# Layer-1 output projection takes its convolution half first; weights of the output and latent stages split at set places; later transposes of maxima; thinner column sums

## The chip, the cores and the metric

One core of one Trainium2 chip. The metric is device time in microseconds (us) of one execution; before the change the median of three runs is 2918.06 us (2916.81 to 2920.32).

## The reference, cut to what matters

Two encoder layers over 2048 tokens of width 1024. What the change touches is layer 1: the latent projections with a norm, eight heads of attention over all tokens, and the output projection of two normed halves, then a layer norm and a gated embedding. (What the program calls the convolution half is the second half of the projection's rows; in layer 1 it holds the result `yd` of the gated chunks.)

```python
cq, ckv, kr, du, dv, z = _split(x @ w_in, ODD_SIZES)
q = (rms_norm(cq, q_norm) @ w_uq).reshape(Bn, S, C_HEADS, C_NOPE + C_ROPE)
kv = (rms_norm(ckv, kv_norm) @ w_ukv).reshape(Bn, S, C_HEADS, C_NOPE + C_V)
...
yc = mla_attention(q_nope, q_rope, k_nope, k_rope, v)      # softmax over all 2048 keys
yd = chunked_spatial_gate(jax.nn.gelu(du), jax.nn.gelu(dv), v_ln_g, v_ln_b, w_s, b_s)
y = jnp.concatenate([rms_norm(yc, c_norm), rms_norm(yd, d_norm)], axis=-1) * jax.nn.silu(z)
...
h = layer_norm(DEEPNORM_ALPHA * x + y @ w_out, post_ln_g[i], post_ln_b[i])
x = h + jax.nn.sigmoid(h @ ple_gate[i]) * (p[i] @ ple_proj[i])
```

## The kernel before, in words

Every large product is made of three matmuls on operands that are split into a high and a low part (`mm3`, lines 77 to 79; for the embedding lines 89 to 91). `split` (lines 67, 68) makes the parts: ScalarE (ACT) copies the high part, and VectorE (DVE) or GpSimd (POOL) subtracts to get the low part. The program runs in five stages: layer-0 projections with windowed attention (0 to 715 us of the span), `phase_out(0)` (to about 1125), `phase_c` (the layer-1 projections, to 1681), `phase_d` (attention, 1681 to 2451) and `phase_out(1)` (to the end).

**Latents** (`part_m`, from 1345 us). Eight small weight tiles (`wuq` six times, `wuk`, `wuv`) are loaded and split before the loop over four latent blocks, whose ScalarE work (lines 1003 to 1005) frees the PSUM buffers `pl` that TensorE (PE) fills.

**Attention** (`phase_d`). 32 blocks (8 heads, 4 chunks of 512 queries), called 0 to 31 here, each with 16 key steps `kb`. A step is three score matmuls into `pst`, one matmul `pm` (line 1166) for the maxima of the block after next, and two value matmuls (`px` line 1216, `py` line 1217) four steps behind; no values run at `kb` 4 and two pairs run at `kb` 5. ACT makes the exponential and `ph`, DVE the low part `pl` (line 1289) and the maximum over `pm` (line 1167), POOL adds `ph` into `acc` (line 1295). At `kb` 2 (`MAX_AT`) the maxima of the next block are transposed (`pmt`, line 1176), through a buffer of the same two-deep PSUM ring `C` that `pm` uses. At `kb` 15 the sums are read back and inverted (`rec`, lines 1252, 1253). In eight blocks a weight tile for the output stage is split at `kb` 13. PE follows the order written out here (`manual_schedule`); a scheduler sets that of the other engines, and each engine is in order.

**Output stage** (`phase_out(1)`). For each of 16 tiles of 128 tokens: `fetch` loads parts of the attention result (`yc`, `ycm`, `rec`) and the finished second half (`ou1`); `prep` (lines 604 to 615) joins and scales the first half, sums its squares over features (`colsum`, line 517: one matmul per 128 columns against a 128x128 tile of ones) and takes the root (`rms`, lines 99 to 105 on one element per row); `first` (from line 617) projects both halves, attention half first, and DVE adds them to `ox` (line 626), then layer norm (POOL lines 634, 635); `second` transposes (`pht`, line 648) and makes `pp` and `pg` (line 89). `ycm`, `rec`, weight tiles `wraw` and `praw` share a ring `rr` of three buffers. `prep(0)` is called at `kb` 2 of the last block, and the last two tiles of `w_out` and all eight of `ple_gate` are loaded around the end of attention.

Once attention is over `ps_open("pse")` lays PSUM out anew with three buffers in ring `C`.

Of the kernel before, what the change touches and what calls it, by code (L numbers as in the profile page):

```python
# [20 lines left out]
P = 128  # L21
# [6 lines left out]
EPS = 1e-6  # L28
BIG = 1e35
LAG = 4  # L30
MAX_AT = 2
SUM_AT = 9
WEIGHT_AT = 13
START_AT = 2
VW = 130
ATTEND = 4000
# [17 lines left out]
class Builder:  # L54
# [20 lines left out]
    def mm3(self, ps, ah, al, bh, bl, start, stop):  # L75
        mm = self.nc.tensor.matmul
        mm(ps, ah, bh, start=start, stop=False)  # L77
        mm(ps, ah, bl, start=False, stop=False)  # L78
        mm(ps, al, bh, start=False, stop=stop)  # L79

    def mm3s(self, ps, a, b, cols):

# [473 lines left out]
    def phase_out(self, layer, es=None, wo=None, w_out=None, w_pr=None, right=None):  # L556
# [8 lines left out]
        w_out = w_out or []  # L565
        wo = wo + self.out_rings(es, f"ow{layer}", range(len(wo), 4), right)
# [3 lines left out]
        xs, us, att, last = {}, {}, {}, {}  # L570
        OU = 3

        def fetch(t):
# [25 lines left out]
        def prep(t):  # L599

            if layer == 0:
                return
            yc, more, rec, sz = att.pop(t)
            u = us[t][0] = of.tile([P, 2, 4, P], F32R, name="ou0", tag="ou", bufs=OU)
            for a in range(2):
                nc.gpsimd.tensor_tensor(yc, yc, more[:, a], ALU.add)
            nc.vector.tensor_tensor(rec, yc, rec, ALU.mult)
            sq = more[:, 0]
            nc.scalar.activation(sq, rec, AF.Square)
            nc.vector.tensor_tensor(sz, rec, sz, ALU.mult)  # L610
            nc.gpsimd.tensor_tensor(sq[:, 0:2], sq[:, 0:2], sq[:, 2:4], ALU.add)
            nc.gpsimd.tensor_tensor(sq[:, 0], sq[:, 0], sq[:, 1], ALU.add)
            self.split(u[:, 0], u[:, 1], sz)
            self.colsum(ss[:, 0, t:t + 1], sq[:, 0], self.psC("cs"))
            self.rms(rs, ss, 0, slice(t, t + 1))

        def first(t):
            x, u = xs[t], us.pop(t)
            for h in range(2):
                for n in range(2):  # L620
                    ns = slice(n * 512, (n + 1) * 512)
                    ps = self.psA("py")
                    for k in range(4):
                        wh, wl = w_out[4 * h + k]
                        self.mm3(ps, u[h][:, 0, k], u[h][:, 1, k], wh[:, ns], wl[:, ns], k == 0, k == 3)
                    last[0] = nc.vector.scalar_tensor_tensor(x[:, ns], ps, rs[:, h, t:t + 1], x[:, ns],
                                                             ALU.mult, ALU.add)
            st = self.cp.tile([P, 20], F32, name="ost", tag="ost", bufs=3)
            for n in range(2):
                nc.vector.bn_stats(st[:, 6 * n:6 * n + 6], x[:, n * 512:(n + 1) * 512])  # L630
            nc.vector.bn_aggr(st[:, 12:14], st[:, 0:12])
            self.rsqrt(self.cp, st[:, 15:16], st[:, 13:14], 1.0, 0.5 * EPS, 1)
            nc.vector.tensor_scalar(x, x, st[:, 12:13], st[:, 15:16], ALU.subtract, ALU.mult)  # L633
            nc.gpsimd.tensor_tensor(x, x, lng, ALU.mult)  # L634
            nc.gpsimd.tensor_tensor(x, x, lnb, ALU.add)
# [41 lines left out]
                    self.dma(d["x1T"][ch, :, a, 4 * k4:4 * k4 + 4, tc_], xt[:, a])  # L677

        if right:
            fetch(0)  # L680
            fetch_x(0)
            w_out = w_out + self.out_weights(wo, I["w_out"][layer], range(len(w_out), 8))
            lng, lnb = self.out_norm(of, layer)
            prep(0)
            yield
            first(0)
            yield
            left = Ring(es, tc, f"ox{layer}l", 2)
            xr.pools += left.pools
        else:  # L690
            wp = self.out_rings(es, f"op{layer}", range(1))
# [82 lines left out]
    def phase_c(self):  # L774
# [191 lines left out]
        def part_m():  # L966
            ms = ExitStack()
            sp = ms.enter_context(tc.tile_pool(name="cm", bufs=1))
            lp, wl, qn, latp = lw
            wq = [None] * 6  # L970
            ring = Ring(ms, tc, "cmq", 6)
            for j in range(6):
                wq[j] = self.load_weight(rr, ring, I["w_uq"][j], f"wuq{j}").rearrange("p a (k m) -> p a k m", m=P)
            wk = self.load_weight(rr, Ring(ms, tc, "cmk", 1), I["w_uk"], "wuk").rearrange("p a (j m) -> p a j m", m=P)
            wv = self.load_weight(rr, Ring(ms, tc, "cmv", 1), I["w_uv"], "wuv")

            def st():
                return tr.tile([P, CH], F32, name="mst")
# [6 lines left out]
            def latents(ch):  # L985
# [7 lines left out]
                for b in range(4):  # L993
# [11 lines left out]
                    nc.scalar.activation(ps[:, lkv], ps[:, lkv], AF.Square, scale=128 ** -0.5, accum_out=sq[:, 0, 1:2])  # L1005
                    nc.gpsimd.tensor_copy(tok[:, 416:432], tok[:, 400:416])
                    nc.gpsimd.tensor_copy(tok[:, 432:448], tok[:, 384:400])
                    self.rsqrt(lp, sq[:, 1], sq[:, 0], 1.0, EPS, 2)
                    for i, cols in enumerate((lq, lkv)):
                        nc.vector.scalar_tensor_tensor(tok[:, cols], tok[:, cols], sq[:, 1, i:i + 1], qn[:, cols],  # L1010
                                                       ALU.mult, ALU.mult)
# [157 lines left out]
    def mla_max_end(self, blk):  # L1169
        nc, c = self.nc, self.c  # L1170
        h, qc = divmod(blk, 4)
        mx = self.mx.pop(blk)
        m = self.cp.tile([P, 4], F32, name="mxr", tag="mxr", bufs=2)
        nc.vector.tensor_reduce(m, mx, AX.X, ALU.max)
        ps = self.psC("pmt")
        nc.tensor.transpose(ps[0:4, 0:P], m, c["ident"])
        mt = self.cp.tile([4, P], F32R, name="mt", tag="mt", bufs=2)
# [13 lines left out]
    def phase_d(self):  # L1191
# [58 lines left out]
        def reciprocals(h, qc, rec):  # L1250
# [5 lines left out]
        weights, after = [], []  # L1256
        steps = chain(self.out_weight(out_wo, self.i["w_out"][1], range(6), after),
                      self.out_weight(out_wp, self.i["ple_proj"][1], range(2), after))
        with tc.manual_schedule(engines={mybir.EngineType.PE}):
            for blk in range(NBLK):  # L1260
                h, qc = divmod(blk, 4)
                qh, ql, kh, kl = self.mla_qk[h % 2]
                qs = slice(qc * CH, (qc + 1) * CH)
                loads = blk in range(6, 28, 3)
                if loads:
                    after.append(old[4])
                    next(steps)
                if blk == NBLK - 3:
                    right.close()
                    self.output = self.phase_out(1, out_es, out_wo, weights[:6], weights[6:], "right")  # L1270
# [6 lines left out]
                for kb in range(16):  # L1277
                    with tc.high_priority(100) if blk == 0 and kb < LAG else ExitStack():
# [27 lines left out]
                        if old is not None:  # L1306
                            if kb == LAG - 1:
                                finish(*old[:4])
                            if kb == SUM_AT - 2:
                                hl = sums(old[4], nc.gpsimd)  # L1310
                            if kb == SUM_AT:
                                rec = total(*old[:2], hl)
                            if kb == 15:
                                with tc.issue_after(behind.ins):
                                    reciprocals(*old[:2], rec)
                        if loads and kb == WEIGHT_AT:
                            with tc.issue_after(ex.ins), tc.issue_after(behind.ins):
                                weights.append(next(steps))
                old = (h, qc, x, y, acc)
            while queue:  # L1320
                values()
            finish(*old[:4])
            hl = sums(old[4], nc.vector)
            self.c_bufs = 3
            self.ps_open("pse")
# [102 lines left out]
```

## Time and profile before

| | before |
|---|---|
| median of three runs | 2918.06 us (2916.81 to 2920.32) |
| profiled execution | 2919.13 us, span 2917.3 us, mean granted clock 0.987 |
| PE busy | 2830.8 us (97%) |
| DVE / ACT / POOL busy | 68% / 45% / 37% |
| chain that ended last | PE 83%, DVE 6%, DMA 6% |

The span is the profiled time from the first instruction to the last; 1.8 us of the execution lie around it. Granted clock 1.00 stands for 2.4 GHz of PE and 0.50 for 1.2 GHz. With PE busy nearly all the time, the rest to be had is what PE waits for, the stretches at the lower clock, and the work itself.

### The profile page before, as it was taken

What the parts mean: (1) busy time and instruction counts of PE and PEld (TensorE: products, weight loads), DVE (VectorE), ACT (ScalarE), POOL (GpSimd) and SP (SyncE); (2) the same over time, 40 slices, a digit from 0 to 9 for tenths busy, and PEclk for the clock granted to TensorE, in tenths of its full rate; (3) what the DMA queues carried; (4) which work ended last, traced back from release to release, by engine and by line L of the source; (5) the groups of instructions that cost most, each with busy time, mean ns of one, the idle gap of its engine ahead of it and who ended that gap; (6) DMA issues with size and microseconds to landing.
All of it is one profiled execution on the core that took longest, in us unless ns stands there. A gap on an engine that the chain in (4) does not pass through costs nothing.

```text
span 2917.3 us, 38322 instructions
## 1 busy us (share of the span) xinstructions
PE 2830.8 (97%) x12808; PEld 2300.1 (79%) x12808; DVE 1993.4 (68%) x3957; ACT 1323.9 (45%) x2475; POOL 1092.1 (37%) x831
## 2 busy tenths in 40 slices
PE   8999999999999999999999999999999998999998
PEld 7888888887788888888888877777777775777777
DVE  3788457886744544455765689999898986655554
ACT  3545335544211112334442388888888885111111
POOL 0011000112311111120103078898989887333332
PEclk9999999999999999999999999999999998999999
DMA  7654365544544346325783233313332233433331
GB/s 231 183 141 141 126 195 162 144 123 147 184 128 124 116 140 241 99 70 188 265 290 80 73 84 75 83 35 73 93 84 56 53 95 103 110 103 115 98 116 40
DMA packets 316598, 365.26 MB, mean 125 GB/s; under 512 B 33248, under 2 KB 244368, under 8 KB 311280
## 3 DMA queue, kind: packets, MB, share of 16 engines
q1 hardware_dynamic: 288752, 333.38, 40.0%
q10 hardware_dynamic: 27648, 29.43, 2.9%
q8 instruction: 101, 1.65, 0.2%
q14 instruction: 97, 0.79, 0.1%
HBM read 238.19 MB, written 124.53 MB: 124 GB/s over the span
## 4 chain that ended last, share of the span: by engine, by line
PE 83%; DVE 6%; DMA 6%; ACT 2%; issue 2%; SPq 1%; POOL 1%; ACTq 0%; DVEq 0%; POOLq 0%
PE pg L89 7%; PE pa L78 6%; PE pa L79 6%; PE pa L77 6%; PE pg L91 4%; PE py L77 4%; PE pst L1281 4%; PE pst L1282 3%; PE py L78 3%; PE pst L1283 3%; PE pm L1166 3%; PE px L1216 3%; PE py L79 3%; PE py L1217 3%; PE pc L79 3%; PE pc L78 3%
## 5 line engine op out<-in xcount | busy, mean ns | idle before, releaser
L1295 POOL TENSOR_TENSOR acc<-acc,ph 128x512 f32<-128x512 f32 x448 | 583.1, 1302 | 52.7 <-ACT ph L1287 23.8
L1289 DVE TENSOR_TENSOR pl<-pst,ph 128x512 fp32r<-128x512 f32 x512 | 348.3, 686 | 62.5 <-ACT ph L1287 45.4
L1167 DVE TENSOR_REDUCE mx<-pm 128x1 f32<-128x512 f32 x512 | 348.5, 682 | 32.6 <-PE pm L1166 28.2
L77 PE MATMUL pa<-xh,w 128*128 128x512 f32 x832 | 327.9, 394 | 6.2 <-ACT xh L67 6.2
L78 PE MATMUL pa<-xl,w 128*128 128x512 f32 x832 | 328.7, 395 | 0.5 <-DVE xl L68 0.5
L1284 ACT ACTIVATE pst<-pst 128x512 f32<-128x512 f32 x512 | 296.3, 583 | 69.9 <-PE pst L1283 38.9
L79 PE MATMUL pa<-xh,w 128*128 128x512 f32 x832 | 327.7, 394 | 0.0
L1287 ACT ACTIVATE ph<-pst 128x512 fp32r<-128x512 f32 x512 | 301.0, 597 | 29.6 <-POOL acc L1295 0.4
L77 PE MATMUL py<-wh,ou 128*128 128x512 f32 x512 | 208.8, 408 | 19.4 <-ACT ou L67 7.8
L1281 PE MATMUL pst<-mqh,mkh 97*128 97x512 f32 x512 | 206.9, 404 | 10.9 <-DVE pl L1289 10.7
L1216 PE MATMUL px<-ph,mv 128*128 128x512 f32 x512 | 207.6, 405 | 3.0 <-ACT ph L1287 3.0
L634 POOL TENSOR_TENSOR ox<-ox,ln_g 128x1024 f32<-128x1024 f32 x32 | 77.0, 2405 | 355.7 <-DVE ox L633 301.8
L658 ACT ACTIVATE osg<-pg 128x512 f32<-128x512 f32 x64 | 38.3, 598 | 374.7 <-PE pg L91 369.7
L78 PE MATMUL py<-wl,ou 128*128 128x512 f32 x512 | 206.4, 403 | 0.0
L1282 PE MATMUL pst<-mql,mkh 96*128 96x512 f32 x512 | 205.3, 401 | 0.0
L1283 PE MATMUL pst<-mqh,mkl 96*128 96x512 f32 x512 | 204.8, 400 | 0.0
L1217 PE MATMUL py<-pl,mv 128*66 128x512 f32 x512 | 204.1, 399 | 0.6 <-DVE pl L1289 0.6
L1166 PE MATMUL pm<-mkh,mqh 96*128 96x512 f32 x512 | 203.0, 397 | 0.2 <-ACT mt L1178 0.2
L89 PE MATMUL pg<-wh,oht 128*128 128x512 f32 x512 | 201.0, 392 | 0.9 <-ACT oht L67 0.9
L79 PE MATMUL py<-wh,ou 128*128 128x512 f32 x512 | 201.4, 400 | 0.0
L89 PE MATMUL pg<-wl,oht 128*128 128x512 f32 x512 | 200.1, 391 | 0.0
L77 PEld LDWEIGHTS pa<-xh,w 128*128 128x128 f32 x832 | 156.9, 189 | 37.1 <-ACT xh L67 6.9
(377 smaller groups left out, 6269.4 us busy)
## 6 DMA issues: line engine op xcount, KB each, us to landing
ou<-u SPq DMA_DIRECT2D x96, 256.0 KB
qw<-q SPq DMA_DIRECT2D x64, 256.0 KB
x1T<-oxt SPq DMA_DIRECT2D x64, 256.0 KB
cx<-x1T SPq DMA_DIRECT2D x16, 1024.0 KB
q<-st SPq DMA_DIRECT2D x32, 256.0 KB
u<-ua SPq DMA_DIRECT2D x32, 256.0 KB
wraw<-in_w_out SPq DMA_DIRECT2D x16, 512.0 KB
ox<-in_x SPq DMA_DIRECT2D x16, 512.0 KB
```

The costliest lines, as they stand in the source:

```text
L77: mm(ps, ah, bh, start=start, stop=False)
L78: mm(ps, ah, bl, start=False, stop=False)
L79: mm(ps, al, bh, start=False, stop=stop)
L89: mm(ps, a[:, 0, k], b[k][part][:, cols], start=k == 0 and part == 0, stop=False)
L1167: nc.vector.tensor_reduce(self.mx[blk][:, b, kc:kc + 1], ps, AX.X, ALU.max)
L1216: mm(x, v[:, kb, 0:P], ph, start=kb == 0, stop=kb == 15)
L1281: mm(ps, kh[0:97, ks], qh[0:97, qs], start=True, stop=False)
L1282: mm(ps, kh[0:96, ks], ql[0:96, qs], start=False, stop=False)
L1284: ex = nc.scalar.activation(ps, ps, AF.Exp, scale=scale)
L1287: nc.scalar.activation(ph, ps, AF.Copy)
L1289: behind = nc.vector.tensor_tensor(pl, ps, pf, ALU.subtract)
L1295: nc.gpsimd.tensor_tensor(acc, acc, pf, ALU.add)
```

## The change

- The transposes of maxima move from `kb` 2 to 5, the reciprocals from `kb` 15 to 14, the weight splits from `kb` 13 to 11; `mt` has one buffer instead of two.
- `colsum` multiplies by two columns of the ones and not by 128, so each output is 2 wide.
- `prep` writes the sum of squares to a tile `sqs` of its own; `colsum` and `rms` of layer 1 move from `prep` into `first`, between the halves; `first` takes the second half first in layer 1.
- The last two tiles of `w_out` are split in blocks 29 and 30 at `kb` 11; `prep(0)` is issued after the last block.
- The eight small latent weights are loaded ahead of everything else in `part_m`; one pair is split after each latent block of the first chunk.

```diff
-MAX_AT = 2
+MAX_AT = 5
 SUM_AT = 9
-WEIGHT_AT = 13
+REC_AT = 14
+WEIGHT_AT = 11
...
-            self.nc.tensor.matmul(ps[:, bl], src[:, bl], self.c["ones"], start=True, stop=True)
-        self.nc.vector.tensor_copy(out, ps.rearrange("p (b m) -> p b m", m=P)[:, 0:n, 0])
+            self.nc.tensor.matmul(ps[:, 2 * b:2 * b + 2], src[:, bl], self.c["ones"][:, 0:2], start=True, stop=True)
+        self.nc.vector.tensor_copy(out, ps[:, 0:2 * n].rearrange("p (b m) -> p b m", m=2)[:, :, 0])
...
+            sqs[t] = of.tile([P, P], F32, name="sqs", tag="sqs", bufs=1)
             nc.scalar.activation(sq, rec, AF.Square)
             nc.vector.tensor_tensor(sz, rec, sz, ALU.mult)
             nc.gpsimd.tensor_tensor(sq[:, 0:2], sq[:, 0:2], sq[:, 2:4], ALU.add)
-            nc.gpsimd.tensor_tensor(sq[:, 0], sq[:, 0], sq[:, 1], ALU.add)
+            nc.gpsimd.tensor_tensor(sqs[t], sq[:, 0], sq[:, 1], ALU.add)
             self.split(u[:, 0], u[:, 1], sz)
-            self.colsum(ss[:, 0, t:t + 1], sq[:, 0], self.psC("cs"))
-            self.rms(rs, ss, 0, slice(t, t + 1))
...
-            for h in range(2):
+            for h in (0, 1) if layer == 0 else (1, 0):
+                if layer == 1 and h == 0:
+                    with tc.issue_after(last[1].ins):
+                        self.colsum(ss[:, 0, t:t + 1], sqs.pop(t), self.psC("cs"))
+                    self.rms(rs, ss, 0, slice(t, t + 1))
...
         if right:
+            lng, lnb = self.out_norm(of, layer)
+            yield
             fetch(0)
             fetch_x(0)
-            w_out = w_out + self.out_weights(wo, I["w_out"][layer], range(len(w_out), 8))
-            lng, lnb = self.out_norm(of, layer)
+            yield
             prep(0)
...
+            raws = [rr.tile([P, 1024], F32, name="wur") for _ in range(3)]
+            wq, wkv, cuts = [], [], []
             for j in range(6):
-                wq[j] = self.load_weight(rr, ring, I["w_uq"][j], f"wuq{j}").rearrange("p a (k m) -> p a k m", m=P)
...
+                self.dma(r, I["w_uq"][j])
+                cuts.append((t, r))
...
             for _ in latents(0):
-                pass
+                with tc.issue_after(behind[0].ins), tc.issue_after(behind[1].ins):
+                    for t, r in cuts[:2]:
+                        self.split(t[:, 0], t[:, 1], r)
+                del cuts[:2]
...
-                loads = blk in range(6, 28, 3)
+                loads = blk in range(6, 28, 3) or blk in (NBLK - 3, NBLK - 2)
...
-                            if kb == 15:
+                            if kb == REC_AT:
...
             finish(*old[:4])
+            with tc.issue_after(behind.ins):
+                next(self.output)
             hl = sums(old[4], nc.vector)
             self.c_bufs = 3
             self.ps_open("pse")
```

On PE, steps `kb` 2 and 3 of an attention block before (first fence, the transpose follows `pm` of `kb` 2) and steps `kb` 4 and 5 now (second fence); `pst` are scores, `px` and `py` values.

```order
L1166 MATMUL pm<-mkh_14444,mqh_14436 128x512
L1176 MATMUL pmt<-ident,mxr 4x128
L1216 MATMUL px<-ph_17212,mv_13674 128x512
L1217 MATMUL py<-pl_17213,mv_13674 66x512
L1281 MATMUL pst<-mqh_13543,mkh_13551 128x512
```

```order
L1236 MATMUL py<-pl_17194,mv_13637 66x512
L1310 MATMUL pst<-mqh_13506,mkh_13514 128x512
L1311 MATMUL pst<-mql_13510,mkh_13514 128x512
L1312 MATMUL pst<-mqh_13506,mkl_13518 128x512
L1185 MATMUL pm<-mkh_14407,mqh_14399 128x512
L1310 MATMUL pst<-mqh_13506,mkh_13514 128x512
L1311 MATMUL pst<-mql_13510,mkh_13514 128x512
L1312 MATMUL pst<-mqh_13506,mkl_13518 128x512
L1185 MATMUL pm<-mkh_14407,mqh_14399 128x512
L1195 MATMUL pmt<-ident,mxr 4x128
L1235 MATMUL px<-ph_17211,mv_13637 128x512
L1236 MATMUL py<-pl_17212,mv_13637 66x512
```

The transpose moved three steps back in its block; the step ahead of it now has no value matmuls.

On DVE in the last block before: work of `prep(0)` (`ss`, `rsq`, `rs`) stands between the low parts `pl` of attention.

```order
L1289 TENSOR_TENSOR pl_23018<-pst,ph_23017 128x512
L518 COPY ss_9899<-cs 128x1
L99 TENSOR_SCALAR rsq<-ss_9899 128x1
L100 TENSOR_SCALAR rsq<-rsq 128x1
L101 TENSOR_SCALAR rs_9898<-rsq 128x1
L1289 TENSOR_TENSOR pl_23029<-pst,ph_23028 128x512
L103 TENSOR_TENSOR rsq<-rs_9898 128x1
L104 SCALAR_TENSOR_TENSOR rsq<-rsq 128x1
...
L104 SCALAR_TENSOR_TENSOR rsq<-rsq 128x1
L1289 TENSOR_TENSOR pl_23041<-pst,ph_23040 128x512
```

Now, on DVE after the last `pl` of attention (`acs` splits the last sums, `ou` is the low part of the first half of tile 0):

```order
L1318 TENSOR_TENSOR pl_23225<-pst,ph_23224 128x512
L608 TENSOR_TENSOR rec_23043<-yc,rec_23043 128x512
L612 TENSOR_TENSOR szt<-rec_23043,szt 128x512
L69 TENSOR_TENSOR acs<-acc,acs 128x512
L69 TENSOR_TENSOR ou_23247<-szt,ou_23247 128x512
L630 SCALAR_TENSOR_TENSOR ox_23051<-py,rs_9898,ox_23051 128x512 x2
L519 COPY ss_9899<-cs 128x1
L100 TENSOR_SCALAR rsq<-ss_9899 128x1
```

All of `prep(0)` on DVE and ACT moved behind the last `pl`; in the last two blocks only `pl`, `rec` and what belongs to attention stand on DVE.

On PE from the end of attention now (before, the first `py` read the first half of tile 0, and the sum `cs` of a tile stood a whole `first` ahead of that tile's matmuls). `ou_23048` is the second half of tile 0, `ou_23247` its first half, `ou_23428` the second half of tile 1; where "..." stands the 24 matmuls of a half go on.

```order
L1236 MATMUL py<-pl_23225,mv_14416 66x512
L78 MATMUL py<-wh_19421,ou_23048 128x512
...
L80 MATMUL py<-wh_22491,ou_23048 128x512
L518 MATMUL cs<-ones,sqs 128x2
L78 MATMUL py<-wh_16088,ou_23247 128x512
...
L80 MATMUL py<-wh_17749,ou_23247 128x512
L1259 MATMUL psum<-acs,ones 128x512
L1260 MATMUL psum<-acs,ones 128x512
L78 MATMUL py<-wh_19421,ou_23428 128x512
```

The half that needs no work of `prep` comes first, and the sum `cs` of a tile lies between its own halves.

## Rows read from the trace of the kernel before

**Rows 1.** Waits of PE, whole span: waiter, releaser, us in total, times, longest.

```profile
PE cs L517 <- POOL ycm L612: 17.5, 6, 5.3
PE pst L1281 <- DVE pl L1289: 10.7, 4, 5.8
PE pmt L1176 <- DVE mx L1167: 8.1, 19, 0.6
PE py L77 <- ACT ou L67: 7.8, 4, 2.0
PE pl L77 <- ACT pl L1005: 5.4, 2, 3.9
```

**Rows 2.** Stretches: length, busy us of PE, PEld, DVE, ACT, POOL, granted clock, DMA.

```profile
1731.00:2340.00 609.00, 601.45 (x2575) 458.22 (x2574) 553.28 (x914) 533.43 (x970) 545.22 (x427) 1.00 0.30 67
2387.80:2451.20 63.40, 50.70 (x176) 35.83 (x174) 37.64 (x61) 44.24 (x82) 52.41 (x43) 0.81 0.32 86
2451.20:2540.00 88.80, 77.27 (x320) 62.24 (x321) 59.16 (x134) 17.02 (x27) 36.96 (x22) 0.92 0.42 117
2540.00:2911.80 371.80, 352.58 (x1571) 287.84 (x1569) 204.23 (x542) 51.64 (x92) 112.83 (x72) 0.98 0.35 97
```

**Rows 3.** Timeline of the latents, ACT and PE: start, length, ..., idle before.

```profile
1354.86 0.42 ACT L67 ACTIVATE wuq<-wuq3r 128x256 fp32r<-128x256 f32 x1 [2.87 <-DMA wuq3r<-in_w_uq]
1364.91 0.71 PE L77 MATMUL pl<-wl,cx 128*128 128x416 f32 x1 [3.95 <-ACT pl L1005]
```

**Rows 4.** The line of the maxima (DVE 1167): one of those who waited for it.

```profile
  PEld pmt L1176: 18.2, 23
```

**Rows 5.** Timeline of steps 4 and 5 of an attention block.

```profile
1761.56 0.69 DVE L1167 TENSOR_REDUCE mx<-pm 128x1 f32<-128x512 f32 x1 [0.70 <-PE pm L1166]
1762.07 0.39 PE L1166 MATMUL pm<-mkh,mqh 96*128 96x512 f32 x1
1762.30 0.39 PE L1216 MATMUL px<-ph,mv 128*128 128x512 f32 x1
```

**Rows 6.** Timeline of blocks 30 and 31.

```profile
2396.77 0.69 DVE L607 TENSOR_TENSOR rec<-yc,rec 128x512 f32<-128x512 f32 x1 [3.72 <-DMA rec<-rec]
2398.85 0.80 PE L1281 MATMUL pst<-mqh,mkh 97*128 97x512 f32 x1 [2.61 <-DVE pl L1289]
2417.23 0.15 DVE L518 COPY ss<-cs 128x1 f32<-128x1 f32 x1
2426.15 0.70 DVE L105 SCALAR_TENSOR_TENSOR rs<-rsq,rs 128x1 f32<-128x1 f32 x1
2426.28 0.80 PE L1281 MATMUL pst<-mqh,mkh 97*128 97x512 f32 x1 [5.78 <-DVE pl L1289]
```

**Rows 7.** A stretch behind the wait of 2.61 us: length, PE busy, granted clock.

```profile
2398.80:2405.60 6.80, 6.72 (x15) 0.52 0.91 243
```

**Rows 8.** POOL's groups in attention: busy, mean ns of one, idle before.

```profile
L1295 POOL TENSOR_TENSOR acc<-acc,ph 128x512 f32<-128x512 f32 x448 | 583.1, 1302 | 52.7 <-ACT ph L1287 23.8 <-POOL acc L1295 0.4
L68 POOL TENSOR_TENSOR acs<-acc,acs 128x512 fp32r<-128x512 f32 x31 | 40.4, 1304 | 3.0 <-ACT acs L67 3.0
```

**Rows 9.** Weights `wraw` from 2380 us: gate loads, POOL's splits (min/median/max ns, first and last).

```profile
L73 SPq DMA_DIRECT2D wraw<-in_ple_gate x8: 332/339/464, 2411.7 to 2484.7; - x8
L68 POOL TENSOR_TENSOR wl<-wraw,wh x5: 2338/2405/2408, 2423.3 to 2489.6; 128x1024 fp32r<-128x1024 f32 x5
```

**Rows 10.** Timeline of the output stage on PE: a column sum, the first gate matmul.

```profile
2486.26 0.80 PE L517 MATMUL cs<-ones,ycm 128*128 128x128 f32 x2 [5.32 <-POOL ycm L612]
2495.78 0.39 PE L89 MATMUL pg<-wh,oht 128*128 128x512 f32 x1
```

**Rows 11.** Timeline of a run of column sums: weight loads and matmuls.

```profile
714.98 1.75 PEld L517 LDWEIGHTS cs<-ones,sqb 128*128 128x128 f32 x14
715.21 3.73 PE L517 MATMUL cs<-ones,sqb 128*128 128x128 f32 x32
```

**Rows 12.** A step of the root on DVE from 2451.6 us (min/median/max ns).

```profile
L103 DVE TENSOR_TENSOR rsq<-rs x45: 147/159/2395, 2465.8 to 2859.4; 128x1 f32<-128x1 f32 x45
```

More of the change, by code (lines that the diff above doesn't have):

```diff
@@ L78, in mm3 @@
         mm(ps, ah, bl, start=False, stop=False)
-        mm(ps, al, bh, start=False, stop=stop)
+        return mm(ps, al, bh, start=False, stop=stop)
     def mm3s(self, ps, a, b, cols):
@@ L564, in phase_out @@
         wo = wo or []
-        w_out = w_out or []
-        wo = wo + self.out_rings(es, f"ow{layer}", range(len(wo), 4), right)
+        w_out = [] if w_out is None else w_out
+        wo = self.out_wo = wo + self.out_rings(es, f"ow{layer}", range(len(wo), 4), right)
         kw = {"side": right} if right else {}
@@ L569, in phase_out @@
         xr = Ring(es, tc, f"ox{layer}", 1 if right else 3, right)
-        xs, us, att, last = {}, {}, {}, {}
+        xs, us, att, sqs, last = {}, {}, {}, {}, {}
         OU = 3
@@ L624, in first @@
                         wh, wl = w_out[4 * h + k]
-                        self.mm3(ps, u[h][:, 0, k], u[h][:, 1, k], wh[:, ns], wl[:, ns], k == 0, k == 3)
+                        last[1] = self.mm3(ps, u[h][:, 0, k], u[h][:, 1, k], wh[:, ns], wl[:, ns], k == 0, k == 3)
                     last[0] = nc.vector.scalar_tensor_tensor(x[:, ns], ps, rs[:, h, t:t + 1], x[:, ns],
@@ L969, in part_m @@
             lp, wl, qn, latp = lw
-            wq = [None] * 6
-            ring = Ring(ms, tc, "cmq", 6)
+            raws = [rr.tile([P, 1024], F32, name="wur") for _ in range(3)]
+            wq, wkv, cuts = [], [], []
             for j in range(6):
-                wq[j] = self.load_weight(rr, ring, I["w_uq"][j], f"wuq{j}").rearrange("p a (k m) -> p a k m", m=P)
-            wk = self.load_weight(rr, Ring(ms, tc, "cmk", 1), I["w_uk"], "wuk").rearrange("p a (j m) -> p a j m", m=P)
-            wv = self.load_weight(rr, Ring(ms, tc, "cmv", 1), I["w_uv"], "wuv")
+                t = sp.tile([P, 2, 256], F32R, name=f"wuq{j}")
+                r = raws[j // 4][:, 256 * (j % 4):256 * (j % 4 + 1)]
+                self.dma(r, I["w_uq"][j])
+                cuts.append((t, r))
+                wq.append(t.rearrange("p a (k m) -> p a k m", m=P))
+            for j, nm in enumerate(("w_uk", "w_uv")):
+                t = sp.tile([P, 2, 512], F32R, name=nm)
+                r = raws[2][:, 512 * j:512 * (j + 1)]
+                self.dma(r, I[nm])
+                cuts.append((t, r))
+                wkv.append(t)
+            wk, wv = wkv[0].rearrange("p a (j m) -> p a j m", m=P), wkv[1]
+            behind = {}
             def st():
@@ L1009, in latents @@
                     for i, cols in enumerate((lq, lkv)):
-                        nc.vector.scalar_tensor_tensor(tok[:, cols], tok[:, cols], sq[:, 1, i:i + 1], qn[:, cols],
-                                                       ALU.mult, ALU.mult)
+                        behind[1] = nc.vector.scalar_tensor_tensor(tok[:, cols], tok[:, cols], sq[:, 1, i:i + 1],
+                                                                   qn[:, cols], ALU.mult, ALU.mult)
                     pt = self.psC("plt")
@@ L1176, in mla_max_end @@
         nc.tensor.transpose(ps[0:4, 0:P], m, c["ident"])
-        mt = self.cp.tile([4, P], F32R, name="mt", tag="mt", bufs=2)
+        mt = self.cp.tile([4, P], F32R, name="mt", tag="mt", bufs=1)
         nc.scalar.activation(mt, ps[0:4, 0:P], AF.Copy, scale=-1.0)
@@ L1254, in reciprocals, with out_steps @@
             self.dma(d["rec"][h, qs].rearrange("(p j) -> p j", j=4), rec[:, 0])
-        weights, after = [], []
-        steps = chain(self.out_weight(out_wo, self.i["w_out"][1], range(6), after),
-                      self.out_weight(out_wp, self.i["ple_proj"][1], range(2), after))
+        w_out, w_pr, after = [], [], []
+        def out_steps():
+            for out, rings, src, ks in ((w_out, out_wo, self.i["w_out"][1], range(6)),
+                                        (w_pr, out_wp, self.i["ple_proj"][1], range(2)),
+                                        (w_out, None, self.i["w_out"][1], range(6, 8))):
+                for w in self.out_weight(rings or self.out_wo, src, ks, after):
+                    if w:
+                        out.append(w)
+                    yield
+        steps = out_steps()
         with tc.manual_schedule(engines={mybir.EngineType.PE}):
@@ L1263, in phase_d @@
                 qs = slice(qc * CH, (qc + 1) * CH)
-                loads = blk in range(6, 28, 3)
+                if blk == NBLK - 3:
+                    right.close()
+                    self.output = self.phase_out(1, out_es, out_wo, w_out, w_pr, "right")
+                    next(self.output)
+                loads = blk in range(6, 28, 3) or blk in (NBLK - 3, NBLK - 2)
                 if loads:
@@ L1317, in phase_d @@
                             with tc.issue_after(ex.ins), tc.issue_after(behind.ins):
-                                weights.append(next(steps))
+                                next(steps)
                 old = (h, qc, x, y, acc)
@@ L1322, in phase_d @@
             finish(*old[:4])
+            with tc.issue_after(behind.ins):
+                next(self.output)
             hl = sums(old[4], nc.vector)
```

5 lines of the change are left out of this document (1 added, 4 removed).

## The prediction

> **What bounds the kernel now.** I read the page first: TensorE (PE) is busy for 2830.8 of the 2917.3 us. Time can come from three places only: less work on PE, waits of PE, and stretches at the lower clock. The list of PE's waits tells who holds it up [rows 1], and the table of stretches tells how much a stage loses [rows 2]. In attention up to block 27 PE is busy for 601.45 of 609.00 us at a clock of 1.00, so it loses some 7.6 us there. From block 30 to the end of attention, 63.40 us, it is idle for 12.7 us, and the clock of 0.81 takes another 0.19 x 63.4 = 12.0: 24.7 us lost, 38.7 of work. In the output stage the first 88.8 us lose 11.5 + 0.08 x 88.8 = 18.6, the other 371.8 us lose 19.2 + 0.02 x 371.8 = 26.6: 45.2 together. The clock falls behind waits: after the one of 2.61 us [rows 6] the next 6.80 us ran at 0.52 [rows 7], which is the level of 1.2 GHz, so a wait of this size costs its length and some 3.3 us more. The waits of up to 0.6 us in attention [rows 1] leave the clock at 1.00 [rows 2].
>
> The sum is made against the profiled execution, 2919.1 us, which lies 1.1 us above the median of the runs.
>
> **Latents: -5.** ScalarE (ACT) stands in order behind weights that have not landed, 2.87 us for one alone, and PE then waits 3.95 us for a PSUM buffer that ACT should have freed [rows 3]; all such waits come to 5.4 us [rows 1]. The change issues the eight loads ahead of everything and places each pair of splits behind ACT's work of a latent block, so nothing of the block stands behind them. The splits are as many as before and lie beside the matmuls of the latent blocks. I take 5, the waits less a remainder, and nothing for the clock; ends: 0 (another load is late instead) and 8.
>
> **Maxima: -10.** At step 2 the transpose wants the PSUM buffer of `pm` from step 1, and VectorE (DVE), late from the reciprocals at the block's start, has not read it. The matmuls waited 8.1 us [rows 1], their weight loads 18.2 [rows 4]; I take 10, near the first, because PE works on while a load waits. At step 5 the buffer is that of step 4. DVE read it from 1761.56 to 1762.25, and PE's next place after `pm` of step 5 was 1762.30 [rows 5]: 0.05 us to spare, after a DVE wait for PE, so DVE had caught up. That margin is thin, because step 4 has no values. Moving the reciprocals to step 14 gives DVE one step more. If the margin fails, one DVE reduction of 0.69 us per block over 30 blocks is 20 us, which is the bad end (+10 on balance); the good end is -18. Moved weight splits and the single `mt` are hidden: POOL, ACT and DVE are busy for 545, 533 and 553 of 609 us [rows 2], and without that cover a POOL split costs 2.4 us [rows 9].
>
> **Blocks 30 and 31: -21.** `prep(0)` stands in the in-order queues here. DVE waited 3.72 us for the load of `rec`, and PE then 2.61 us for `pl`; the root (one element per row) ran from 2417.23 to 2426.85 on DVE, and PE waited 5.78 us behind it [rows 6]. All of that moves behind the last block, so these waits and the clock they cost go. POOL is late next: 30 additions at 1.30 and two `acs` at 1.30 [rows 8] are 41.7 us, and a weight split at 2.4 [rows 9] makes 44.1, against PE's 38.7. The values don't need these sums, and seven buffers of `ph` let POOL lag by some steps, so I put the pair of blocks at 42.4, between the two: 63.4 - 42.4 = 21. Ends: 25 (PE alone) and 13 (POOL sets the pace and its waits bring one fall of the clock). The two weight tiles in blocks 29 and 30 add a split each, beside matmuls.
>
> **Output stage: -27 of 45.** What PE waits for is `cs` behind POOL, 17.5 us, and `py` behind ACT's `ou`, 7.8 us [rows 1]. The first case is seen at 2486.26: `cs` of a tile stands on PE ahead of matmuls that don't need it, 5.32 us idle [rows 10]. Now the half that needs no `prep` comes first, which gives the sum and the split 24 matmuls, 24 x 0.23 = 5.6 us [rows 5], more; and `sqs` frees a buffer of the load ring sooner. In the first stretch I leave 9 of 18.6: POOL's lag of 2 to 3 us at the end of attention delays `acs`, behind which DVE has `ou` of tile 0, plus one wait for a load, plus one fall of the clock. The rest loses 26.6 in waits of about 2 us that return with the ring of three; I leave a third, 9. Gain 9.6 + 17.4 = 27. Ends: 10 (the loads are as late as before) and 44.
>
> **Column sums: 0.** 32 instructions took 3.73 us, 0.117 us each, while the weight loads came every 1.75/14 = 0.125 us without a gap [rows 11]. A thinner result shortens the streaming; the 128 columns of weights stay, and the loads alone fill the run. For all 128 such instructions the ends are 0 and 15 us, the whole run; I take 0, by the row of the loads. The Trainium skill (TensorE: Matmul & The Clock Gate, LDWEIGHTS) gives a load as its columns divided by 1.2, an estimate of 107 ns here, so it speaks against this edit: by that the sum would gain 128 x 0.010 = 1.3 us more. The run of 0.117 agrees.
>
> Sum: -5 - 10 - 21 - 27 + 0 = -63, so 2856 us. With every end at its best it is -95 (2824; with free column sums 2809), with every end at its worst -13 (2906).
>
> **Rivals.**
> 1. *The gate weights come late.* All eight loads of `ple_gate` now follow the end of attention; before they ran from 2411.7 to 2484.7 [rows 9], the first of them ahead of that end. They pass the ring of three beside `ycm` and `rec`. The first `pg` stood at 2495.78 [rows 10], 44.6 us after attention; now it is due after some six halves, about 36 us. If it comes no earlier than before, PE waits 8.6 us and the clock costs 3.3: 2868. For it: POOL's split of 2.4 us per tile [rows 9], and its lag. Against: DMA is busy for 0.42 of that stretch [rows 2].
> 2. *The margin at step 5 fails.* The maxima then give +10 in place of -10: 2876. For it: 0.05 us [rows 5]. Against: DVE had waited for PE there.
> 3. *Thin sums pay.* Were PE's loads hidden, up to 15 us: 2841. Against: the row of the loads [rows 11].
> 4. *Slower: the root in the middle of `first`.* It now stands on DVE between the halves, ahead of the addition of the first half and the split of `pht` that `pg` needs. From `cs` to that `pg` PE has 24 + 12 matmuls and 8 transposes, about 9.3 us; additions and splits take 2.8 of that on DVE, so it decides when the root takes over 6.5 us. It took 9.6 beside POOL's additions [rows 6]. Then each tile waits 3.1 us and pays 3.3 for the clock: 16 x 6.4 = 102, so 2958. Against: a step has a median of 159 ns [rows 12], which makes 2 us for twelve, and POOL is busy for a third of the stage; for it: single steps of 2395 ns, the length of a POOL operation. The Trainium skill (SBUF — State Buffer, Terms, "shared port pair") says that VectorE and GpSimd share a pair of ports under an exclusive lock, held for a whole instruction; by that rule any step with two inputs can be stalled, and the long steps in the row agree.
>
> **How the numbers follow.** The forecast has 0.5 (its own range 2842 to 2870), rival 1 0.2, rival 2 0.14, rival 3 0.11, rival 4 0.05. The forecast and rivals 1 to 3 lie between 2828 and 2884 with 8 in 10 of the chance when their own spread of some 12 us is counted; that is the range. About 0.2% (6 us) can be told from no change. Only rival 4 is slower; of its 0.05 the chance leaves 0.04 slower and 0.01 in a mild form that just uses up the gain, and 0.01 comes from all ends at their worst: faster 0.94, same 0.02, slower 0.04.
>
> **What would show it.** Right: no `pmt` wait in PE's list; no wait for `pl` above 1 us in the last two blocks, which take about 42 us; the output stage from the last value to the last matmul in some 433 us, with `cs` and `ou` below 10 us together; no `pl` wait in the latents; sums still about 0.11 us apart. Wrong: PE waits for `pg` weights or `ou` of over 5 us after attention, `pmt` waiting at its new place, or long root steps ahead of a PE wait in each tile.

## The result and the profile after

The changed kernel takes 2886.2 us (median, 2884.56 to 2887.82); the kernel before, timed beside it, 2919.2. The ratio is 0.9888 (95% interval 0.9871 to 0.9905): 33 us faster. The forecast was 2856 us with a range of 2828 to 2884, so the sign was right, the size about half, and the time lies 2 us outside the range.

The page after: span and busy times.

```profile
span 2885.3 us, 38365 instructions
...
PE 2820.2 (98%) x12808; PEld 2290.2 (79%) x12808; DVE 2014.4 (70%) x3957; ACT 1322.6 (46%) x2475; POOL 1091.2 (38%) x833
```

The waits of PE after, over the whole span (waiter, releaser, us in total, times, longest). Lines have moved: `cs` is line 518, the projections 78 to 80, the DVE addition 630.

```profile
PE py L78 <- DVE ox L630: 10.8, 7, 4.4
PE py L78 <- ACT ou L68: 7.5, 1, 7.5
PE pa L78 <- ACT xh L68: 7.0, 2, 5.0
PE py L78 <- DMA ou<-u: 6.6, 2, 4.0
PE pm L1185 <- DVE mx L1186: 3.5, 5, 1.4
PE py L80 <- DMA ou<-u: 2.6, 1, 2.6
PE psum L1259 <- ACT acs L68: 2.0, 1, 2.0
...
PE psum L1260 <- POOL acs L69: 1.6, 1, 1.6
```

Against [rows 1], the 17.5 us of `cs` are gone, and so are the 8.1 us of `pmt` for `mx`. New in layer 1 are one wait of 7.5 us for `ou` (the longest was 2.0) and waits of 6.5 us for loads of `ou` (the other 2.6 us lie in layer 0, as 3.2 us did before), and PE now stands at `psum` in the last block for 3.6 us where it stood 0.7. One wait of 1.8 us of `pmt`, for another releaser (`mxr`) and ahead of block 1, is left.

The stretches after that answer to [rows 2]: attention up to block 27; blocks 30 and 31; the first 88 us behind them; the rest up to the last matmul.

```profile
1731.00:2340.00 609.00, 604.57 (x2584) 458.46 (x2583) 552.84 (x919) 534.85 (x975) 549.42 (x429) 1.00 0.30 67
2381.10:2431.60 50.50, 44.19 (x174) 31.61 (x173) 26.91 (x45) 40.19 (x76) 48.82 (x39) 0.93 0.20 55
2431.60:2520.00 88.40, 68.79 (x273) 54.21 (x273) 59.19 (x133) 19.11 (x27) 42.86 (x27) 0.86 0.51 139
2520.00:2880.20 360.20, 356.69 (x1620) 292.88 (x1618) 244.89 (x562) 52.09 (x95) 108.73 (x72) 1.00 0.36 103
```

Read as before (idle time plus what the clock took), the first stretch of the output stage now loses 19.6 + 0.14 x 88.4 = 32 us where it lost 18.6, and the rest loses 3.5 us where it lost 26.6. So the stage became quiet in its steady part and worse at its start. In the two profiles, by the first score matmul of a block, the last value matmul and the last matmul of all (one profile of each kind; the experiments tell how far such a row can be trusted):

| stretch | before, us | after, us | difference | forecast |
|---|---|---|---|---|
| start to block 1 (latents lie here) | 1707.75 | 1704.67 | -3.1 | -5 |
| block 1 to block 30 (maxima) | 680.1 | 676.4 | -3.6 | -10 |
| blocks 30 and 31 | 63.3 | 50.3 | -13.0 | -21 |
| last value to last matmul | 460.5 | 448.5 | -11.9 | -27 |

**Blocks 30 and 31.** The timeline of POOL, ACT and PE in the last two blocks (start, us, engine, line, op; in brackets idle time before and releaser):

```profile
2399.37 2.40 POOL L69 TENSOR_TENSOR wl<-wraw,wh 128x1024 fp32r<-128x1024 f32 x1
2406.96 11.31 POOL L1324 TENSOR_TENSOR acc<-acc,ph 128x512 f32<-128x512 f32 x9
2416.45 0.63 ACT L68 ACTIVATE acs<-acc 128x512 fp32r<-128x512 f32 x1
2417.14 0.80 PE L1259 MATMUL psum<-acs,ones 128*128 128x512 f32 x1 [2.03 <-ACT acs L68]
2418.23 1.26 POOL L69 TENSOR_TENSOR acs<-acc,acs 128x512 fp32r<-128x512 f32 x1
2419.54 0.79 PE L1260 MATMUL psum<-acs,ones 128*128 128x512 f32 x1 [1.61 <-POOL acs L69]
```

Block 30 takes 19.54 us, all of it PE work; block 31 takes 30.8. POOL runs without a pause from the weight split to past the wait for its `acs` and falls behind. PE reaches `psum`, which wants the sums of block 30 at step 9 of block 31, and waits for POOL's `acs` with all later scores queued behind it. So some values did need these sums, by way of PE's order.

**The start of the output stage.** PE, ACT and DVE after attention:

```profile
2447.62 0.60 PE L78 MATMUL py<-wh,ou 128*128 128x512 f32 x1 [3.98 <-DMA ou<-u]
2466.26 2.30 DVE L106 SCALAR_TENSOR_TENSOR rs<-rsq,rs 128x1 f32<-128x1 f32 x1
2469.48 0.80 PE L78 MATMUL py<-wh,ou 128*128 128x512 f32 x1 [4.37 <-DVE ox L630]
2471.07 1.06 ACT L68 ACTIVATE wh<-wraw 128x1024 fp32r<-128x1024 f32 x1 [5.36 <-DMA wraw<-in_ple_gate]
2479.96 0.69 DVE L608 TENSOR_TENSOR rec<-yc,rec 128x512 f32<-128x512 f32 x1 [2.49 <-DMA rec<-rec]
2483.43 0.80 PE L78 MATMUL py<-wh,ou 128*128 128x512 f32 x1 [7.45 <-ACT ou L68]
2494.97 0.50 PE L80 MATMUL py<-wh,ou 128*128 128x512 f32 x1 [2.56 <-DMA ou<-u]
```

The second half of tile 1 has not landed when PE wants it (3.98 us). Then the addition `ox` is late (4.37 us): it stands on DVE behind the root of tile 1, which runs from 2458.05 to 2468.56 us, between other work and with steps of over 2 us. Then tile 2's `rec` comes late, its load issued at 2471.5, after the last of the eight gate weights, and `ou` of tile 2 with it (7.45 us). Over the 6.4 to 6.6 us behind these three waits the granted clock was 0.73, 0.57 and 0.59. The first gate matmul starts 67 us after attention, where it was 44.6 [rows 10].

**Column sums.** The run of 32 instructions, now with two columns:

```profile
716.22 3.63 PE L518 MATMUL cs<-ones,sqb 128*128 128x2 f32 x32
```

It was 3.73 us with 128 columns [rows 11]: 3 ns less for each instruction. The 32 weight loads took 3.77 us before and 3.76 now, one every 0.115 us in both.

### The profile page after: what moved, and what is told of

It reads as the page before. It is cut to its first block, busy times and chain, and to the rows that moved or that the text cites. A ratio compares the mean times of both kernels' runs of the same rounds, so it can differ in the third digit from the quotient of the medians.

```text
span 2885.3 us, 38365 instructions
## 1 busy us (share of the span) xinstructions
PE 2820.2 (98%) x12808; PEld 2290.2 (79%) x12808; DVE 2014.4 (70%) x3957; ACT 1322.6 (46%) x2475; POOL 1091.2 (38%) x833
```

## Experiments

Eight kernels undo one part or relieve one suspected cost, then four join what helped, two do one part by itself on the kernel before, and one varies the fastest. In every batch the kernel before was timed beside; ratios are to it. The changed kernel itself was timed in the first batch only (0.9888), so small differences from it are read from the ratios.

**The late transposes undone** (`MAX_AT = 2`, one line).

> The changed kernel with the transposes of maxima back at step 2; all else as changed. Theory (late transposes are worth what the blocks lost): blocks 1 to 29 take 23.2 to 23.5 us again in place of some 22.95, pmt waits for mx some 0.5 us in about 20 blocks, and the whole is 4 to 10 us slower than the changed kernel's 2886 us: 2890 to 2896. Rival (the shorter blocks came from the reciprocals at step 14, which take DVE's lateness away from step 2): no pmt waits, and 2884 to 2888 us.

2889.5 us, ratio 0.9891 (0.9876 to 0.9906): 3 us above the changed kernel by the medians, 1 us by the ratios, inside the intervals. The profile shows the mechanism: in the stretch from block 1 to block 30 (waits of PE) the transposes wait again,

```profile
PE pmt L1195 <- DVE mx L1186: 8.7, 20, 0.8
```

and the stretch takes 682.2 us in place of 676.4. The rival (that the reciprocals alone do it) falls. Of the profile's 6 us the whole showed little, since this run began attention 5 us earlier. And this pair lies at the ends of its kinds: over all 17 profiles the stretch takes 675.7 to 682.1 us with late transposes (14 kernels) and 680.1 to 682.2 with early ones (3), on average 3 us apart.

**Wide column sums again** (both lines of `colsum` as before).

> The changed kernel with 128-column sums again. Theory (the weight loads set the pace of a run of sums): the run of 32 sums at about 716 us takes 3.7 us as before, against 3.63 changed, and the whole is within 2 us of 2886. Rival (thin sums are part of the gain): 2889 to 2898 us, with the sums slower where they stand singly.

2882.4 us, 0.9869 (0.9854 to 0.9885), no slower than the changed kernel, which speaks against the rival, and 4 us below it, which the theory did not expect; the run of 32 took 3.73 us. The thin sums are worth nothing that can be measured.

**Attention half first again.**

```diff
-            for h in (0, 1) if layer == 0 else (1, 0):
+            for h in (0, 1):
```

> The changed kernel with the attention half first again in layer 1; the sums of squares keep their own tile and the column sum stands ahead of the first half. Theory A (the steady waits of the output stage fell because the sums left the ring of three early): from 100 us after attention on PE still loses under 1 us per tile, only the start is worse by 5 to 15 us, 2888 to 2902 us in all. Rival B (they fell because the other half stands first): waits of about 2 us come back every tile or every third, 20 us and more, 2905 to 2930 us.

2883.4 us, 0.9871 (0.9854 to 0.9887). From 90 us after attention on PE lost nothing at all:

```profile
2520.00:2877.20 357.20, 357.20 (x1628) 294.10 (x1626) 221.41 (x552) 52.49 (x95) 115.78 (x75) 1.00 0.36 104
```

Rival B falls. Theory A was right that the steady part stays quiet. Its loss of 5 to 15 us at the start came to 4 us (36 in place of 32) and was made up behind it, and the whole lies below its range: the half order by itself, with the sum in `first`, is worth nothing that can be measured.

**Latent loads as before.**

> The changed kernel with the loads and splits of the latent weights as before. Theory (the 7 us gained by the last latent block were given back before attention starts): PE waits of about 4 and 1.7 us come back near 1349 and 1361 us, attention starts within 2 us of 1681.8, and the whole stays within 2 us of 2886. Rival (the gain is kept and something else is lost there): attention starts 4 to 7 us later and the whole takes 2890 to 2894 us.

2888.1 us, 0.9888 (0.9873 to 0.9902). The waits for `pl` came back, 5.1 us in 2. Attention started at 1681.6 us, as the theory said, but block 1 at 1707.0, and one profile tells little here: over all 17 profiles block 1 starts at 1695.8 to 1704.7 us with the new loads (13 kernels) and at 1702.9 to 1707.8 with the old ones (4), on average 6 us apart, while the first kind spreads by 9 us and the second by 5. The medians differ by 2 us, the ratios not at all. The latents themselves tell more: from the 40th `pl` matmul (near 1347 us) to the last, PE takes 107.3 to 110.2 us in all 13 and 114.3 to 117.2 in all 4. So 7 us are gained there; at the start of attention 2.5 of them are left on average, and why the rest goes is open.

**The column sum back in `prep`**, with the squares in the ring's buffer, and beside it with their own tile:

```diff
+            self.colsum(ss[:, 0, t:t + 1], sqs.pop(t), self.psC("cs"))
+            self.rms(rs, ss, 0, slice(t, t + 1))
...
-                if layer == 1 and h == 0:
-                    with tc.issue_after(last[1].ins):
-                        self.colsum(ss[:, 0, t:t + 1], sqs.pop(t), self.psC("cs"))
-                    self.rms(rs, ss, 0, slice(t, t + 1))
```

> The changed kernel with the column sum and the root of layer 1 back in prep and the squares back in the buffer of the load ring, as before the change; half order, late prep of tile 0 and the rest as changed. Theory (the ring buffer held until PE's column sum made the steady waits): from 90 us after attention on PE loses 20 us or more again in place of 9, 2897 to 2910 us. Rival (the place of the sum does not matter, another part freed the stage): under 12 us lost there, 2880 to 2892 us.

> As the run beside it, but the squares keep their own tile outside the ring. If the held ring buffer alone made the steady waits, they stay away: under 12 us lost from 90 us after attention on, 2880 to 2892 us. If it was that PE met the sum ahead of matmuls that don't need it, 15 us or more come back as waits of cs for POOL: 2892 to 2910 us.

2901.6 us (0.9935, 0.9919 to 0.9951) and 2901.1 us (0.9931, 0.9915 to 0.9948): 13 to 15 us of the 33 go, with either buffer. So the ring's buffer was not what mattered; the place of the sum and of the root, which move together here, was. The stretches of the second kernel's output stage, start and rest:

```profile
2430.90:2520.00 89.10, 73.43 (x290) 58.26 (x290) 66.00 (x141) 19.21 (x27) 42.37 (x27) 0.87 0.51 150
2520.00:2898.80 378.80, 362.56 (x1603) 294.93 (x1601) 215.47 (x552) 52.68 (x95) 108.74 (x72) 0.97 0.33 95
```

The rest loses 16 us idle and 11 to the clock again. But the waits there (first two lines) are not those of the kernel before (last two):

```profile
PE py L78 <- DVE ox L628: 11.5, 6, 3.6
PE cs L518 <- POOL sqs L614: 3.8, 1, 3.8
PE cs L517 <- POOL ycm L612: 12.2, 5, 3.8
PE py L77 <- ACT ou L67: 5.9, 3, 2.0
```

The 15 us or more of `cs` that were expected did not come. All six additions had themselves waited on DVE, 2.7 to 10.5 us, for the load of the residual `x`:

```profile
2604.46 1.41 DVE L628 SCALAR_TENSOR_TENSOR ox<-py,rs,ox 128x512 f32<-128x512 f32 x2 [10.48 <-DMA ox<-x]
```

The scheduler orders PE and the loads of this stage anew for each kernel. So a loss of the old size came back, by another wait, and how the sum's place leads to late loads of `x` is not shown.

**`prep` of tile 0 inside the last block again** (a second `next(self.output)` step at `kb` 2, none behind the block).

> The changed kernel with prep of tile 0 issued inside the last block again, with its loads. Theory (in-order work of prep ahead of attention's low parts made blocks 30 and 31 long, and POOL's backlog is what is left): the last block takes 33 to 40 us in place of 30.8, the start of the output stage gains 2 to 4 us, 2887 to 2897 us. Rival (POOL alone sets the last block, so more work for DVE and ACT hides): block 31 within 1.5 us of 30.8 and the whole 2881 to 2886 us.

2880.2 us, 0.9865 (0.9851 to 0.988): not slower, if anything 6 us faster. Its stretches: blocks 30 and 31, start, rest.

```profile
2374.00:2435.50 61.50, 49.31 (x174) 33.72 (x173) 33.78 (x50) 44.03 (x81) 55.05 (x44) 0.86 0.34 94
2435.50:2525.00 89.50, 76.03 (x323) 60.91 (x323) 66.49 (x147) 16.71 (x26) 35.31 (x23) 0.94 0.43 116
2525.00:2872.00 347.00, 344.38 (x1570) 283.31 (x1568) 236.55 (x540) 50.28 (x92) 109.01 (x72) 1.00 0.36 103
```

The theory is right on the last block (36.9 us) and wrong on the whole, as the output stage is shorter by 12 us (436.6) and not by 2 to 4; the rival is wrong on the block and 1 us off on the whole. Blocks 30 and 31 take 11 us more than in the changed kernel, so what late prep takes out of them it puts behind them. The two profiles are 8 us apart, and 7 of these lie ahead of block 1.

**Two of POOL's operations on DVE.**

```diff
-                                hl = sums(old[4], nc.gpsimd)
+                                hl = sums(old[4], nc.vector if blk == NBLK - 1 else nc.gpsimd)
...
-            eng = self.nc.gpsimd if k % 2 and src.shape[0] == D else self.nc.vector
+            eng = self.nc.gpsimd if k % 2 and src.shape[0] == D and not (after and k == 7) else self.nc.vector
```

> The changed kernel with two of POOL's operations on DVE: the low part of the sums of block 30 (1.3 us) and that of the last w_out tile (2.4 us). Theory (POOL's backlog holds PE at psum in block 31): block 31 takes 24 to 28 us in place of 30.8, no wait of psum over 1 us, 2879 to 2884 us. Rival (the wait moves to the ph ring behind POOL's additions): block 31 within 1.5 us of 30.8, 2884 to 2888 us.

2879.9 us, 0.9861 (0.9846 to 0.9876). Block 31 takes 23.2 us in place of 30.8 and no wait of `psum` is over 0.3 us, which shows that POOL's backlog held PE there. Its stretches: blocks 30 and 31, and the start of the output stage.

```profile
2378.50:2421.90 43.40, 41.45 (x174) 30.30 (x173) 28.95 (x47) 39.47 (x76) 41.83 (x33) 1.00 0.25 66
2421.90:2512.00 90.10, 64.88 (x257) 51.31 (x257) 65.49 (x132) 17.17 (x24) 46.99 (x31) 0.83 0.50 134
```

The stage behind gives back 4 of the 7.6 us: it takes 452.5 us. Of the 6 us between the two profiles 4 lie ahead of block 1.

**Joining them.** `halves(1)` loads the second half of tile 1 together with tile 0; the second kernel also places the loads of tile 2 after four of the eight gate weights; the third and fourth have early prep.

> The run with POOL relieved, and the second half of tile 1 loaded together with tile 0's parts, before attention ends. Theory (the first wait after attention is for that load): the wait of 5.3 us for DMA near 8 us after attention falls below 1 us and the whole takes 2872 to 2878 us. Rival (the chain of weight loads for the gate sets when the stage gets going, so each early gain turns into a longer wait for tile 2): that wait is gone, later ones grow by as much, 2878 to 2883 us.

> As the run beside it, and the loads of tile 2 placed after four of the eight gate weights. Theory (tile 2 waits for ring buffers that the gate weights hold): the wait of 7 to 8 us for ou of tile 2 falls below 3 us, the first gate matmul may wait instead by up to 3 us, 2868 to 2877 us. Rival (only the sum of loads counts): the gate weights are then later by as much, and the time is within 3 us of the run beside it.

> POOL relieved, and prep of tile 0 back inside the last block. Theory (prep's work is moved from one place to another, worth nothing net, while POOL's backlog is a cost of its own): the last block takes 28 to 34 us, the output stage 436 to 440 us, and the whole 2873 to 2880 us. Rival (relief and early prep free the same time): 2879 to 2884 us.

> POOL relieved, prep of tile 0 inside the last block, and the second half of tile 1 loaded before attention ends. If the load counts with early prep too, the output stage takes 430 to 436 us and the whole 2868 to 2876 us; if it is hidden there (no wait for that load was seen with early prep), within 2 us of the run with early prep alone.

2874.9, 2873.6, 2876.9 and 2872.2 us (0.9849, 0.9849, 0.9858 and 0.9844, each within 0.0015 or so). The first meets its theory's time, but a wait was exchanged: that for the load was gone, and one of 6.4 us for the addition `ox`, behind the root on DVE, stood in its place; the wait of 7.2 us for `ou` of tile 2 stayed. In the second that wait stayed too, at 8.0 us, although the load of `rec` for tile 2 was issued 24 us after attention in place of 30, and the time is within 3 us of the first, as the rival said. There POOL's addition `yc` of tile 2 had stood 8.6 us for the load of `ycm`, a buffer of the same ring; what sets this wait stays open. The third meets its theory on the whole, with an output stage of 430.0 us, 6 better than expected. In the fourth, inside its range for the whole, the output stage takes 422.6 us, the shortest of all.

**Parts by themselves.** The sum's place alone on the kernel before:

```diff
+            sqs[t] = of.tile([P, P], F32, name="sqs", tag="sqs", bufs=1)
+            nc.gpsimd.tensor_tensor(sqs[t], sq[:, 0], sq[:, 1], ALU.add)
...
-            self.colsum(ss[:, 0, t:t + 1], sq[:, 0], self.psC("cs"))
-            self.rms(rs, ss, 0, slice(t, t + 1))
...
+            if layer == 1:
+                self.colsum(ss[:, 0, t:t + 1], sqs.pop(t), self.psC("cs"))
+                self.rms(rs, ss, 0, slice(t, t + 1))
             for h in range(2):
```

> The kernel before with one part of the change: the squares of layer 1 get their own tile (the tile mt gives up one buffer for the room), and column sum and root move from prep to the start of first; half order, prep of tile 0 and all else as before. Theory (the place of the sum is by itself what frees the output stage): from 90 us after attention on PE loses under 12 us in place of 31, 2896 to 2906 us. Rival (it needs the other parts): 2910 to 2922 us.

2881.5 us, 0.9867 (0.9851 to 0.9884): 40 us, no less than the whole change (33 us) and 15 us beyond the best case expected. Its stretches: blocks 30 and 31, start, rest.

```profile
2387.30:2444.70 57.40, 47.88 (x175) 32.72 (x173) 29.95 (x47) 44.58 (x82) 51.72 (x41) 0.91 0.34 97
2444.70:2534.70 90.00, 82.11 (x357) 66.72 (x357) 64.01 (x151) 18.19 (x28) 38.88 (x24) 0.94 0.47 128
2534.70:2871.90 337.20, 337.15 (x1536) 277.50 (x1534) 208.84 (x539) 49.28 (x90) 109.92 (x72) 1.00 0.36 103
```

The rest of the stage has no wait at all, the start loses 13 us in place of 18.6, and the last two blocks, from which the root has gone, are 6 us shorter. So this part carries the gain, with the attention half first and with `prep(0)` in the last block. Sum and root moved together, and the scheduler's order with them; no run parts the two.

The late transposes and reciprocals alone:

> The kernel before with transposes at step 5 and reciprocals at step 14 alone. Theory (the waits of pmt go, half of them come back as waits of pm): the stretch from block 1 to block 30 takes 675 to 678 us in place of 680.1, the whole 2912 to 2917 us. Rival (the forecast's 10 us): 668 to 672 us there, 2906 to 2911 us.

2917.9 us, 0.9989 (0.998 to 0.9999): 3 us. The waits of PE from block 1 to block 30:

```profile
PE pmt L1176 <- DVE mx L1167: 3.1, 3, 2.4
PE pst L1281 <- DMA mqh<-mrow: 3.1, 4, 1.1
PE pm L1166 <- DVE mx L1167: 2.9, 4, 1.2
```

Neither expectation was met: the stretch took 681.6 us in this profile, no less than before. The many small waits went, and fewer, longer ones came, also for the row of maxima, which is written three steps later.

The attention half first on the fastest kernel so far:

> The kernel with POOL relieved, early prep and early load (2872 us), with the attention half first. Theory (the half order is worth nothing once the sum stands in first): 2869 to 2876 us, the output stage within 4 us of 422.6. Rival (with prep early the other half's cover counts): 2877 to 2885 us.

2869.3 us, 0.9825 (0.9811 to 0.984), the fastest of all kernels, 52 us below the kernel before; its interval overlaps that of the kernel it varies. The time is the theory's, but the output stage took 430.4 us, not within 4 of 422.6. Blocks 30 and 31 differ by 1 us only. What made up for it lies where the edit changes nothing: block 1 started 5 us earlier (1695.8 against 1700.7 us), and blocks 1 to 29 took 676.5 us against 682.1. Whether the half order costs 8 us in the stage here is open.

## Why the prediction was right or wrong

The terms miss by 2, 6, 8 and 15 us in the order of the table, and the whole by 30. The steps that failed are two: that nothing waits for POOL's sums in the last two blocks, and that the work of `prep(0)` is nearly free behind attention.

**Latents, -5.** 7 us in the latents themselves, 3 at block 1 in this pair of profiles, 6 there in the average over all, 0 to 2 in the whole: about right, at the edge of what can be told.

**Maxima, -10.** Mis-sized: 3.6 us in the stretch, 1 and 3 us in the whole in the two experiments. That "0.05 us to spare" would do held for `pmt`, which no longer waits for `mx` in the changed kernel; but I had not asked what `pm` behind it would wait for. 3.5 us of such waits came (the list of waits after), and I had taken more than PE itself had waited, 8.1 us.

**Blocks 30 and 31, -21.** The waits for `pl` went as argued, 13 us were gained, which is the bad end of the term. The failed step is "the values don't need these sums". `psum` stands on PE at step 9 and does. With POOL relieved the two blocks took 43.2 us, so the error of 8 us goes with this one sentence. That this is within 1 us of the 42.4 that I had put is luck in part: PE was busy for 41.45 us there at a clock of 1.00, where I had worked out 38.7 for PE alone, and the rest of the 42.4 was a guess towards POOL's 44.1.

**Output stage, -27.** Two errors that partly cancel. The steady part was to keep 9 of 26.6 us and kept 3.5. The start was to lose 9 us and lost 32: here the step failed that I booked the moved `prep(0)` as a gain in blocks 30 and 31 and charged its new place with only 2 to 3 us of POOL's lag, one load and one fall of the clock. Loads, splits and root that hid beside attention's matmuls now stand at the one place where PE has nothing else to do. Undoing the late prep cost nothing: the start then loses 19 us in place of 32. Three waits of 4 to 7.5 us came, each with a low clock behind it. Two are near rival 1 in kind, loads behind attention, but they sit at `ou`, and that the gate weights cause them is not shown: moving tile 2's loads ahead of half of them did not shorten the wait. The one in the middle is rival 4's, the addition behind the root, in one tile. The start lost 23 us more than the 9 I had left, where rival 1 had put 12.

**And the reason for the steady gain was the wrong one.** I put it to the half that comes first and to the ring's buffer. The experiments show that neither is what counts: with the attention half first nothing is lost, and with an own tile and the other half first but the sum in `prep` 27.6 us are lost again. What counts is the place of the sum and the root: moved alone they bring the gain, moved back they take it. In `prep` the sum of tile t+2 stands right behind `first(t+1)`, so a `second` (and not a `first`) ahead of its own tile's matmuls; now it stands among these, in `first(t+2)`. How that place works is shown for the kernel before only, where PE waits at `cs` for POOL and at `py` for `ou`. In the undone kernels PE waits for additions behind loads of `x`, so the chain there is another and open.

**Column sums, 0.** Right: 0.1 us for a run of 32, and the kernel with wide sums was no slower. The spacing of 0.113 us stayed at that of the loads, 0.115 us before and after; the 0.125 of the prediction had the full length of the last load in it. Rival 3 falls. Rival 2 falls, since `pmt` did not wait for `mx` in attention. Rival 4 falls as a cost in each tile, but not its premise: steps on one element per row that took over 1 us became 28 in the output stage where they had been 7, and at one tile of the start such a root held PE for 4.4 us. In the rest of the stage PE lost 3.5 us in all, behind loads of `x`.

## What to carry to other kernels

Where an in-order engine meets a small result ahead of work that doesn't need it, moving that result past the work can be worth as much as a whole rebuilt stage; try it alone first, and look in the trace whether the waits it was meant to end are those that go. Work that is moved out from under a long stage has to be charged in full where it lands, above all if it lands where the bound engine starts something new. Before a slow engine's sums are called off the path, look where the busy engine's own order reads them.

## What had not been expected

The changed kernel, the one with early prep and the one with POOL relieved have the same order on every compute engine up to the start of attention, and their profiled executions came there at 1681.8, 1674.3 and 1677.4 us. One profile of each kind is no measure for a term of 5 us at the front. And the waits of PE at the start of the output stage replace each other: the load of tile 1 taken away (5.3 us), a wait of 6.4 us for the addition stood in its place.
